# Up-projections of a two-layer decoder trunk: two short matrix products per weight tile or one long one

## The chip, the cores and the metric

The kernel runs on one core of a Trainium2 chip. The metric is the device time of one execution in microseconds, as the median of several. A core has five engines with a queue of instructions each, worked off in order: TensorE (matrix products, and the loading of their stationary operand), VectorE, ScalarE, GpSimd, and SyncE, which here only issues DMAs. Matrix products write to PSUM, which has eight banks of 512 float32 columns on 128 partitions; the other data lie in SBUF.

## The reference

Input is one sequence of 256 tokens with 1024 features, in float32. The trunk is an attention layer, a gated feed-forward layer with a short causal convolution, a second attention layer and a second feed-forward layer, with a final normalisation. The change concerns the feed-forward layers only:

```python
def conv_ffn(h, w_up, conv_w, conv_b, w_down):
    S_ = h.shape[1]
    u = h @ w_up
    up = jnp.pad(u, ((0, 0), (CONV_W - 1, 0), (0, 0)))
    u = conv_b + sum(conv_w[j] * up[:, j:j + S_] for j in range(CONV_W))
    gate, val = jnp.split(u, 2, axis=-1)
    return (jax.nn.silu(gate) * val) @ w_down
...
        x = x + conv_ffn(rmsnorm(x, ffn_norm[l]), w_up[l], conv_w[l], conv_b[l], w_down[l])
```

Here `w_up` is 1024 × 5632 (gate and value, 2816 columns each), `w_down` 2816 × 1024, and the convolution has width 3.

## The kernel before

**Precision.** Each float32 operand of a large product is split into a high part in the matrix unit's rounded float32 format and a low part, the rounded rest. A product is the sum of three: high by high, high by low, low by high. ScalarE makes the high part of a weight (`hi_part`, L177), VectorE the low part by a subtraction (`lo_part`, L185).

**Weights.** They come in 92 units of 128 × 2048 float32, 1 MB each, one DMA per unit from SyncE's queue into one of three buffers (`wr`), from where they are split into one of four pairs of buffers (`wh`, `wl`). `used(i)`, called when the products of unit i are written down, puts the preparation of unit i + 4 on a list: high and low part in two pieces each (four for the first few units of a stage), and after the last low part the DMA for unit i + 3.

**Order.** TensorE's products are written down in the order of the program. Other work is put on a list with due times by `chain(key, (delay, step), ...)`; `tick(ns)` moves a planned clock forward with each product and lets what is due be written down, and `require(key)` writes it down at once where a product needs it. The planned clock is a means to order instructions and nothing that runs on the chip. In the feed-forward layers the framework's scheduler still arranges the instructions of each engine from that order and from their dependences.

**Up-projection.** For each i from 0 to 21 one unit of weights holds, for eight chunks c of 128 input features and two halves j (gate and value), a 128 × 128 block. A step makes 2 × 8 × 3 = 48 products: the weight block is the stationary operand, the input, transposed to features by 256 tokens, the moving one. The result is two halves of 128 × 256, that is one PSUM bank. Steps 0 to 3 (`n_raw`) read the input before it is multiplied by the normalisation's row factors `rb`, and VectorE multiplies their results by `rb` afterwards (`scale`, L714) into an SBUF tile. From step 4 on the input read is the scaled one, `hS`, which `scale_x` makes (L698, L700, L701), and the results are read from PSUM directly. Their banks come from two tags in turn, "u" and "t", of two banks each.

**After the product** (`post`): ScalarE applies the last tap and the bias (`tap2`, L718) into an SBUF tile; VectorE adds the two other taps to it (`taps`, L722 and L724, two of each per step); ScalarE takes the gate's silu (L728), GpSimd multiplies it by the value half (L729), ScalarE and VectorE split the outcome into high and low part (L733, L734). These are the stationary operands of the down-projection, 11 units of weights with products of 512 columns (L588, L589, L593) that accumulate in the four "acc" banks.

The names `turns` and `pairs` are views: a product reads columns t and t + half of its moving operand in turn, and writes them to neighbouring places of PSUM, so that the result lies with the two tokens or features of a pair next to each other as the data are laid out here.

Of the kernel before, what the change touches and what calls it, by code (L numbers as in the profile page):

```python
# [10 lines left out]
AF = mybir.ActivationFunctionType  # L11
ALU = mybir.AluOpType
AX = mybir.AxisListType

P = 128
D = 1024
S = 256
NB = S // P
KC = D // P
# [7 lines left out]
NF = DFF // P  # L27
# [32 lines left out]
def trunk(ctx: ExitStack, tc, x, xw, pos, cpk, fin, sinks, w, out):  # L60
    nc = tc.nc
# [8 lines left out]
    def nm(s):  # L70
        uid[0] += 1
        return f"{s}_{uid[0]}"
# [5 lines left out]
    def spaced(pool, n, dt, tag, name, bufs):  # L78
        return pool.tile([P, n + ROUND], dt, tag=tag, name=name, bufs=bufs)[:, SKIP:SKIP + n]

    def quad(dt=F32R, name="q"):
        return spaced(qd, 4 * S, dt, "q", nm(name), 15).rearrange("p (c t) -> p c t", c=4)

    def mid():
        return wk.tile([P, 512], F32, tag="m2", name=nm("m2"), bufs=6)

    def row3(n=3 * P):
        return wk.tile([P, 3 * P + 8], F32, tag="m3", name=nm("m3"), bufs=8)[:, 4:4 + n]
# [7 lines left out]
    def bank(tag):  # L96
        return ps.tile([P, 512], F32, tag=tag, name=nm(tag), bufs=4 if tag == "acc" else 2)

    def f(ap):
        return ap.bitcast(F32)  # L100
# [7 lines left out]
    def turns(ap):  # L108

        return ap.rearrange("p (a t) -> p t a", a=2)  # L110

    def pairs(ap):
        return ap.rearrange("p (t a) -> p t a", a=2)
# [8 lines left out]
    def run_item(item):  # L122
        put_off.remove(item)
        was, busy[0] = busy[0], True
        item[2]()
        busy[0] = was

    def tick(ns):
        clock[0] += ns
        while put_off and not busy[0]:  # L130
            item = min(put_off, key=lambda t: t[0])
            if item[0] > clock[0]:
                return
            run_item(item)

    def chain(key, *steps, urgent=0):

        def run(k):
            if urgent:
                with tc.high_priority(offset=urgent):  # L140
                    steps[k][1]()
            else:
                steps[k][1]()
            if k + 1 < len(steps):
                put_off.append((clock[0] + steps[k + 1][0], key, lambda: run(k + 1)))
        put_off.append((clock[0] + steps[0][0], key, lambda: run(0)))

    def require(*key):

        while True:  # L150
            mine = [t for t in put_off if t[1] == key]
            if not mine:
                return
            run_item(min(mine, key=lambda t: t[0]))


    wq = {}
# [55 lines left out]
    def used(i):  # L213

        prepare(i + 4)

    def need(i):
        require("w", i)
# [48 lines left out]
    for b in range(NB):  # L267
        t = one.tile([P, NH, HD], F32, name=f"v{b}")
# [12 lines left out]
    def new_hT():  # L281

        return [(quad(), quad()) for _ in range(2)]
# [71 lines left out]
    def hx(hT, c):  # L355
        hi, lo = hT[c // 4]
        return hi[:, c % 4], lo[:, c % 4]
# [306 lines left out]
    def ffn(layer, u_up, u_dn, hT, y, rb, after, tail=None):  # L664
        parts = []

        n_raw = 4
        hS = new_hT()

        def mm(i, up, cs_):  # L670
            need(u_up + i)
            hi, lo = wq[u_up + i]
            for j in range(2):
                o = up[j]
                for c in cs_:
                    if i < n_raw:
                        for b in range(NB):
                            require("x", b, c // 4)
                    else:
                        require("y", c // 2)  # L680
                    s_ = slice((2 * c + j) * P, (2 * c + j + 1) * P)
                    xh, xl = (turns(t) for t in hx(hT if i < n_raw else hS, c))
                    nc.tensor.matmul(pairs(o), hi[:, s_], xh, start=(c == 0), stop=False)  # L683
                    nc.tensor.matmul(pairs(o), hi[:, s_], xl, start=False, stop=False)  # L684
                    nc.tensor.matmul(pairs(o), lo[:, s_], xh, start=False, stop=(c == KC - 1))  # L685
                    tick(3 * 256 / 2.4)

        def scale_x(m):

            c = slice(2 * (m % 2), 2 * (m % 2) + 2)  # L690
            y_, hi, lo = (t[:, c] for t in (y[m // 2], *hS[m // 2]))

            def times():
                for b in range(NB):
                    require("rb", b)
                y4 = y_.rearrange("p c (a t) -> p c a t", a=2)
                r4 = rb.rearrange("p (t a) -> p a t", a=2).unsqueeze(1).to_broadcast([P, 2, 2, P])
                nc.vector.tensor_tensor(out=y4, in0=y4, in1=r4, op=ALU.mult)  # L698

            chain(("y", m), (2000.0 + 1000.0 * m, times), (700.0, lambda: nc.scalar.activation(hi, y_, AF.Copy)),  # L700
                  (600.0, lambda: nc.vector.tensor_tensor(out=lo, in0=y_, in1=f(hi), op=ALU.subtract)))  # L701

        def post(i, up, pq):
            hi, lo = pq[:, 2 * (i % 2)], pq[:, 2 * (i % 2) + 1]
            t = [row3(S) for _ in range(2)]
            gs, h = row3(S), row3(S)
            w0, w1, w2, bb = ([cp[:, CW + (layer * 2 * NF + j * NF + i) * 4 + k:][:, :1] for j in range(2)] for k in range(4))
            us = [mid()[:, :S] for _ in range(2)] if i < n_raw else up

            def scale():  # L710
                for b in range(NB):
                    require("rb", b)
                for j in range(2):
                    nc.vector.tensor_tensor(out=us[j], in0=up[j], in1=rb, op=ALU.mult)  # L714

            def tap2():
                for j in range(2):
                    nc.scalar.activation(t[j], us[j], AF.Identity, scale=w2[j], bias=bb[j])  # L718

            def taps():  # L720
                for j in range(2):
                    nc.vector.scalar_tensor_tensor(out=t[j][:, 1:], in0=us[j][:, :S - 1], scalar=w1[j], in1=t[j][:, 1:],  # L722
                                                   op0=ALU.mult, op1=ALU.add)
                    nc.vector.scalar_tensor_tensor(out=t[j][:, 2:], in0=us[j][:, :S - 2], scalar=w0[j], in1=t[j][:, 2:],  # L724
                                                   op0=ALU.mult, op1=ALU.add)

            def gate():
                nc.scalar.activation(gs, t[0], AF.Silu)  # L728
                nc.gpsimd.tensor_tensor(out=h, in0=gs, in1=t[1], op=ALU.mult)  # L729

            steps = [(200.0, scale), (700.0, tap2)] if i < n_raw else [(200.0, tap2)]
            chain(("p", i), *steps, (400.0, taps), (1600.0, gate),
                  (3400.0, lambda: nc.scalar.activation(hi, h, AF.Copy)),  # L733
                  (450.0, lambda: nc.vector.tensor_tensor(out=lo, in0=h, in1=f(hi), op=ALU.subtract)))  # L734
            parts.append((hi, lo))

        pq = quad()
        ups = [[bank(t)[:, :S] for _ in range(2)] for t in ("u", "acc")]
        for cs_ in (range(4), range(4, KC)):
            for i in range(2):  # L740
                mm(i, ups[i], cs_)
        for i in range(2):
            used(u_up + i)
            post(i, ups[i], pq)
        for m in range(4):
            scale_x(m)
        for i in range(2, NF):
            if i % 2 == 0:
                pq = quad()
            up = bank("acc" if i < 4 else "t" if i % 2 else "u")  # L750
            mm(i, [up[:, :S], up[:, S:]], range(KC))
            used(u_up + i)
            post(i, [up[:, :S], up[:, S:]], pq)

        def wait(i):
            require("p", 2 * i)
            require("p", 2 * i + 1)

        if tail is not None:
            nc.sync.dma_start(fin_t, fin.partition_broadcast(P))  # L760
        dn = Down(u_dn, NF // 2, parts, wait, tail is not None)
        for _ in dn.units(0, NF // 2 - 2):
            pass
        dn.finish(NF // 2 - 2, after, tail)
# [20 lines left out]
    hT = new_hT()  # L785
# [200 lines left out]
    hT = new_hT()  # L986
    y = [quad(F32, "y") for _ in range(2)]
# [13 lines left out]
    def after_f0(b, n):  # L1001
# [3 lines left out]
        raw_feats(b, n, xT_h, ("x", b, n))  # L1005

    ffn(0, U_UP0, U_DN0, hT, y, rb, after_f0)


# [60 lines left out]
    hT = new_hT()  # L1070
    y = [quad(F32, "y") for _ in range(2)]
# [55 lines left out]
    r_t = one.tile([P, 1], F32, name="r_t")  # L1127
    yo = []
    ffn(1, U_UP1, U_DN1, hT, y, rb, after_f1, tail)
    while put_off:  # L1130
        run_item(min(put_off, key=lambda t: t[0]))
# [92 lines left out]
```

## Time and profile before

| | |
|---|---|
| median of 3 runs | 551.83 us (551.73 to 551.88) |
| profiled execution | 551.75 us |
| its span, first to last instruction | 550.0 us |
| mean granted TensorE clock | 0.997 |
| TensorE products busy | 540.9 us, 98% of the span |
| VectorE busy | 423.2 us, 77% |
| ScalarE busy | 371.4 us, 68% |
| GpSimd busy | 117.1 us, 21% |
| DMA | 100.98 MB, 184 GB/s |

A line of the profile names the engine (PE is TensorE's products, PEld its weight loads, DVE VectorE, ACT ScalarE, POOL GpSimd), the program line, the operation and the tiles written and read. Groups give total and mean duration. In a timeline a row begins with start and duration in microseconds, and brackets show how long the engine stood idle before it and what released it. Durations of neighbouring instructions on one engine overlap a little, so the pace of a run of instructions is read from their starts. In the first layer's feed-forward part, products of step 4 begin at about 136.5 us and those of the down-projection at about 233 us; in the second layer these are 389.5 and 486 us.

### The profile page before, as it was taken

To read this page: it belongs to the slowest core of one execution; us is meant where nothing else is said; L and a number is where in the kernel's file an instruction comes from. 1 tells how busy PE (TensorE), PEld (TensorE's weight loads), DVE (VectorE), ACT (ScalarE), POOL (GpSimd) and SP (SyncE) were. 2 spreads that over 40 slices of the span, in tenths; PEclk is the share of its full clock that TensorE was granted. 3 is DMA by queue.
4 is the path that set the end of the run, shared out by engine and by line. 5 is a ranking of instruction groups with operands and counts; after the bars stand their busy time and mean duration, and the time that the engine had idled before them with its cause. 6 is when DMAs were issued, how large, how long until landed. Compare 5 with 4: busy or idle time off the path is not lost.

```text
span 550.0 us, 9980 instructions
## 1 busy us (share of the span) xinstructions
PE 540.9 (98%) x3762; PEld 497.1 (90%) x3762; DVE 423.2 (77%) x901; ACT 371.4 (68%) x732; POOL 117.1 (21%) x156
## 2 busy tenths in 40 slices
PE   9999999999999999999999999999999999999995
PEld 7888888899999999988888887889999999998884
DVE  6799777589798889864468989878888898884414
ACT  6779878579577777754368888677657777764313
POOL 8312001012422333130000121102332332320003
PEclk9999999999999999999999999999999999999998
DMA  8985444432466655566552544242374555666201
GB/s 292 396 285 191 154 153 154 154 130 101 164 229 221 228 197 200 220 230 221 173 217 88 220 153 154 83 148 83 148 265 184 203 200 223 238 240 228 99 0 76
DMA packets 15311, 100.98 MB, mean 184 GB/s; under 512 B 1952, under 2 KB 2080, under 8 KB 3744
## 3 DMA queue, kind: packets, MB, share of 16 engines
q1 hardware_dynamic: 14976, 100.09, 50.2%
q8 instruction: 29, 0.48, 0.3%
q10 hardware_dynamic: 288, 0.26, 0.1%
q14 instruction: 18, 0.15, 0.1%
HBM read 99.30 MB, written 1.05 MB: 182 GB/s over the span
## 4 chain that ended last, share of the span: by engine, by line
PE 87%; DMA 3%; ACT 3%; DVE 3%; issue 1%; POOL 1%; POOLq 0%; DVEq 0%; ACTq 0%
PE acc L588 9%; PE acc L593 9%; PE acc L589 9%; PE u L683 7%; PE u L685 6%; PE u L684 6%; PE t L683 6%; PE t L685 6%; PE t L684 6%; PE acc L366 3%; PE acc L367 3%; PE acc L368 3%; DMA wr<-in_w 3%; DVE wl L185 2%; PE acc L685 2%; PE acc L684 2%
## 5 line engine op out<-in xcount | busy, mean ns | idle before, releaser
L185 DVE TENSOR_TENSOR wl<-wr,wh 128x1024 fp32r<-128x1024 f32 (+1 forms) x190 | 207.2, 1108 | 52.2 <-ACT wh L177 51.7
L177 ACT ACTIVATE wh<-wr 128x1024 fp32r<-128x1024 f32 (+1 forms) x188 | 175.0, 959 | 51.4 <-PE acc L593 43.0
L729 POOL TENSOR_TENSOR m<-m,m 128x256 f32<-128x256 f32 x44 | 71.1, 1617 | 166.7 <-DVE m L724 98.5
L588 PE MATMUL acc<-wh,q 128*128 128x512 f32 x238 | 92.2, 387 | 0.0
L589 PE MATMUL acc<-wl,q 128*128 128x512 f32 x238 | 90.5, 380 | 0.0
L683 PE MATMUL u<-q,wh 128*128 128x256 f32 x320 | 88.3, 277 | 0.0
L684 PE MATMUL u<-q,wh 128*128 128x256 f32 x320 | 88.1, 276 | 0.0
L685 PE MATMUL u<-q,wl 128*128 128x256 f32 x320 | 87.9, 275 | 0.0
L683 PE MATMUL t<-q,wh 128*128 128x256 f32 x288 | 79.2, 275 | 0.0
L684 PE MATMUL t<-q,wh 128*128 128x256 f32 x288 | 79.2, 275 | 0.0
L685 PE MATMUL t<-q,wl 128*128 128x256 f32 x288 | 79.2, 275 | 0.0
L593 PE MATMUL acc<-wh,q 128*128 128x512 f32 x238 | 74.5, 379 | 0.0
L685 PEld LDWEIGHTS u<-q,wl 128*128 128x128 f32 x320 | 61.4, 192 | 0.0
L684 PEld LDWEIGHTS u<-q,wh 128*128 128x128 f32 x320 | 61.4, 192 | 0.0
L683 PEld LDWEIGHTS u<-q,wh 128*128 128x128 f32 x320 | 61.3, 192 | 0.0
L683 PEld LDWEIGHTS t<-q,wh 128*128 128x128 f32 x288 | 55.3, 192 | 0.0
L684 PEld LDWEIGHTS t<-q,wh 128*128 128x128 f32 x288 | 55.3, 192 | 0.0
L685 PEld LDWEIGHTS t<-q,wl 128*128 128x128 f32 x288 | 55.3, 192 | 0.0
L588 PEld LDWEIGHTS acc<-wh,q 128*128 128x128 f32 x238 | 45.0, 189 | 6.7 <-issue 0.9
L593 PEld LDWEIGHTS acc<-wh,q 128*128 128x128 f32 x238 | 45.0, 189 | 6.3
L589 PEld LDWEIGHTS acc<-wl,q 128*128 128x128 f32 x238 | 45.0, 189 | 5.7
L733 ACT ACTIVATE q<-m 128x256 fp32r<-128x256 f32 x44 | 18.1, 415 | 46.6 <-POOL m L729 46.6
(177 smaller groups left out, 1030.1 us busy)
## 6 DMA issues: line engine op xcount, KB each, us to landing
wr<-in_w SPq DMA_DIRECT2D x90, 1024.0 KB, 4.8
first<-in_xw SPq DMA_DIRECT2D x5, 384.0 KB, 5.7
xr<-in_x SPq DMA_DIRECT2D x2, 512.0 KB, 9.7
first<-in_xw SPq DMA_DIRECT2D x1, 768.0 KB, 7.1
fin_t<-in_fin SPq DMA_DIRECT2D x1, 512.0 KB, 5.6
out<-ot SPq DMA_DIRECT2D x1, 512.0 KB, 2.6
first<-in_xw SPq DMA_DIRECT2D x1, 388.0 KB, 3.3
out<-m SPq DMA_DIRECT2D x1, 256.0 KB, 2.0
```

Of the source, the lines that this page charges most:

```text
L177: nc.scalar.activation(wq[i][0][:, c], raws[i][:, c], AF.Copy, **({} if g is None else {"scale": g}))
L185: nc.vector.tensor_tensor(out=wq[i][1][:, c], in0=raws[i][:, c], in1=f(wq[i][0][:, c]), op=ALU.subtract)
L366: nc.tensor.matmul(pairs(o), xh[:, blk(b)], turns(wh), start=(c == 0), stop=False)
L367: nc.tensor.matmul(pairs(o), xh[:, blk(b)], turns(wl), start=False, stop=False)
L588: nc.tensor.matmul(pairs(o), ph[:, blk(b)], turns(hi[:, s_]), start=first, stop=False)
L589: nc.tensor.matmul(pairs(o), ph[:, blk(b)], turns(lo[:, s_]), start=False, stop=False)
L593: nc.tensor.matmul(pairs(o), pl[:, blk(b)], turns(hi[:, s_]), start=False, stop=end)
L683: nc.tensor.matmul(pairs(o), hi[:, s_], xh, start=(c == 0), stop=False)
L684: nc.tensor.matmul(pairs(o), hi[:, s_], xl, start=False, stop=False)
L685: nc.tensor.matmul(pairs(o), lo[:, s_], xh, start=False, stop=(c == KC - 1))
L729: nc.gpsimd.tensor_tensor(out=h, in0=gs, in1=t[1], op=ALU.mult)
L733: (3400.0, lambda: nc.scalar.activation(hi, h, AF.Copy)),
```

## The change

From step 4 on, the moving operand holds the high and the low part of the scaled input side by side: `hS` becomes four tiles of two chunks each, in each chunk 256 high and 256 low columns. For each chunk and half, the high part of the weights meets both in one product of 512 columns, which writes a whole PSUM bank: columns 0 to 255 collect high by high, 256 to 511 high by low. The low part of the weights meets the high input in a product of 256 columns that is added to the first 256. A step has 32 products in place of 48. It takes two banks, one for each half, and the pairs of banks come from "u", "t" and twice from "acc" in turn.

The two halves of a bank have to be summed. ScalarE copies the second 256 columns of both banks to an SBUF tile (`aside`), and VectorE adds the first 256 columns from PSUM to it (`both`). The last tap and the other taps read this tile, where they read PSUM before. Steps 0 to 3 keep their products; the two halves of their scaled result now share one tile of 512 columns, where they had one tile each. The planned clock still moves forward by the same amount for each chunk and half.

```diff
-        hS = new_hT()
+        hS = [quad().rearrange("p c (k t) -> p (c k) t", k=1).rearrange("p (c k) t -> p c k t", k=2) for _ in range(KC // 2)]
+
+        def mm_scaled(i, up):
+            need(u_up + i)
+            hi, lo = wq[u_up + i]
+            for c in range(KC):
+                require("y", c // 2)
+                both = hS[c // 2][:, c % 2]
+                for j in range(2):
+                    s_ = slice((2 * c + j) * P, (2 * c + j + 1) * P)
+
+                    def high():
+                        nc.tensor.matmul(up[j].rearrange("p (k t a) -> p k t a", k=2, a=2), hi[:, s_],
+                                         both.rearrange("p k (a t) -> p k t a", a=2), start=(c == 0), stop=(c == KC - 1))
+
+                    def low():
+                        nc.tensor.matmul(pairs(up[j][:, :S]), lo[:, s_], turns(both[:, 0]), start=False, stop=False)
+
+                    for step in (low, high) if c == KC - 1 else (high, low):
+                        step()
+                    tick(3 * 256 / 2.4)
...
-            y_, hi, lo = (t[:, c] for t in (y[m // 2], *hS[m // 2]))
+            y_, hi, lo = y[m // 2][:, c], hS[m][:, :, 0], hS[m][:, :, 1]
...
-            us = [mid()[:, :S] for _ in range(2)] if i < n_raw else up
+            us = [t[:, j * S:(j + 1) * S] for t in (mid(),) for j in range(2)]
+
+            def aside():
+                for j in range(2):
+                    nc.scalar.activation(us[j], up[j][:, S:], AF.Copy)
+
+            def both():
+                for j in range(2):
+                    nc.vector.tensor_tensor(out=us[j], in0=up[j][:, :S], in1=us[j], op=ALU.add)
...
-            steps = [(200.0, scale), (700.0, tap2)] if i < n_raw else [(200.0, tap2)]
+            steps = [(200.0, scale), (700.0, tap2)] if i < n_raw else [(200.0, aside), (450.0, both), (700.0, tap2)]
...
-            up = bank("acc" if i < 4 else "t" if i % 2 else "u")
-            mm(i, [up[:, :S], up[:, S:]], range(KC))
+            if i < n_raw:
+                up = bank("acc")
+                up = [up[:, :S], up[:, S:]]
+                mm(i, up, range(KC))
+            else:
+                up = [bank(("u", "t", "acc", "acc")[(NF - 1 - i) % 4]) for _ in range(2)]
+                mm_scaled(i, up)
             used(u_up + i)
-            post(i, [up[:, :S], up[:, S:]], pq)
+            post(i, up, pq)
```

More of the change, by code (lines that the diff above doesn't have):

```diff
@@ L675, in mm @@
                 for c in cs_:
[L676 to L680, printed above, removed]
+                    for b in range(NB):
+                        require("x", b, c // 4)
                     s_ = slice((2 * c + j) * P, (2 * c + j + 1) * P)
-                    xh, xl = (turns(t) for t in hx(hT if i < n_raw else hS, c))
+                    xh, xl = (turns(t) for t in hx(hT, c))
                     nc.tensor.matmul(pairs(o), hi[:, s_], xh, start=(c == 0), stop=False)
```

## The prediction

> **What bounds the kernel now.** I read the page first, then the busy time by stage over the two stretches that the change touches (the 18 scaled up-projection steps of each layer), then the timeline of single engines inside them. The rows of stretches give, after the length, the busy time of matrix products, weight loads, VectorE, ScalarE and GpSimd, then TensorE's clock.
>
> ```profile
> PE 540.9 (98%) x3762; PEld 497.1 (90%) x3762; DVE 423.2 (77%) x901; ACT 371.4 (68%) x732; POOL 117.1 (21%) x156
> 136.50:233.00 96.50, 96.50 (x866) 96.50 (x866) 83.56 (x136) 66.39 (x110) 29.45 (x18) 1.00 0.58 208
> 389.50:486.00 96.50, 96.50 (x867) 96.50 (x866) 82.57 (x137) 66.58 (x110) 31.25 (x18) 1.00 0.58 213
> ```
>
> In both stretches TensorE is busy without a gap at full clock and sets the end. VectorE is busy 83.56 of 96.50 us, so it is the next in line. A busy TensorE says little about pace, so the pace comes from starts. First two starts one step apart (48 products of 256 columns), then two starts of down-projection that lie eight weight units, 192 products of 512 columns, apart:
>
> ```profile
> 158.00 0.28 PE L683 MATMUL u<-q,wh 128*128 128x256 f32 x1
> ...
> 163.36 0.28 PE L683 MATMUL t<-q,wh 128*128 128x256 f32 x1
> ...
> 238.22 0.38 PE L588 MATMUL acc<-wh,q 128*128 128x512 f32 x1
> ...
> 279.66 0.38 PE L588 MATMUL acc<-wh,q 128*128 128x512 f32 x1
> ```
>
> A 256-column product costs 5.36 / 48 = 111.7 ns, a 512-column one 41.44 / 192 = 215.8 ns. Two short ones cost 223.4, so one long one in their place is 7.6 ns cheaper. What happens where the two lengths meet shows in two places:
>
> ```profile
> 541.66 0.38 PE L593 MATMUL acc<-wh,q 128*128 128x512 f32 x1
> 541.88 0.27 PE L649 MATMUL u<-wh,q 128*128 128x256 f32 x1
> 541.99 0.28 PE L650 MATMUL u<-wl,q 128*128 128x256 f32 x1
> ...
> 38.00 0.28 PE L459 MATMUL acc<-kd,q 128*128 128x256 f32 x1
> 38.11 0.38 PE L366 MATMUL u<-wh,q 128*128 128x512 f32 x1
> ```
>
> After a long product the next starts 0.22 us later, after a short one 0.11 us later: the length of the earlier product decides, and mixing adds nothing.
>
> **TensorE's term.** Each (chunk, half) of a scaled step had three short products, 335.0 ns. It will have one long and one short, 215.8 + 111.7 = 327.5 ns. That is 7.5 ns, times 16 per step, 18 steps and 2 layers = 576 places: 4.3 us. The columns streamed are the same 768; only a weight load and a product's fixed part go. A step becomes 16 × 327.5 = 5.24 us instead of 5.36. The unknown is the long product's read, which takes the high and the low block of one tile as two runs; all long products of the trace read one block. Bounds: as the down-projection's (215.8), or no cheaper than two short ones (223.4, gain nothing). I take 215.8, since the short products of L649, which read pairs 256 elements apart, keep the same 0.11 us as L683's pairs 128 apart: the read pattern did not matter there.
>
> **What the other engines get.** Each scaled step gains two ScalarE copies out of PSUM and two VectorE additions, and the bias and tap operations read SBUF instead of PSUM. One step of today in VectorE's, ScalarE's and GpSimd's order:
>
> ```profile
> 205.89 0.43 DVE L734 TENSOR_TENSOR q<-m,q 128x256 fp32r<-128x256 f32 x1 [0.68 <-ACT q L733]
> 206.23 0.47 DVE L724 SCALAR_TENSOR_TENSOR m<-t,cp,m 128x254 f32<-128x254 f32 x1
> 206.63 0.47 DVE L722 SCALAR_TENSOR_TENSOR m<-t,cp,m 128x255 f32<-128x255 f32 x1
> 207.02 1.22 DVE L185 TENSOR_TENSOR wl<-wr,wh 128x1024 fp32r<-128x1024 f32 x1
> 208.15 0.47 DVE L724 SCALAR_TENSOR_TENSOR m<-t,cp,m 128x254 f32<-128x254 f32 x1
> 208.54 1.21 DVE L185 TENSOR_TENSOR wl<-wr,wh 128x1024 fp32r<-128x1024 f32 x1
> 209.67 0.48 DVE L722 SCALAR_TENSOR_TENSOR m<-u,cp,m 128x255 f32<-128x255 f32 x1
> 210.83 0.43 DVE L734 TENSOR_TENSOR q<-m,q 128x256 fp32r<-128x256 f32 x1 [0.68 <-ACT q L733]
> ...
> 205.44 0.42 ACT L733 ACTIVATE q<-m 128x256 fp32r<-128x256 f32 x1 [1.29 <-POOL m L729]
> 205.76 1.05 ACT L177 ACTIVATE wh<-wr 128x1024 fp32r<-128x1024 f32 x1
> 206.80 0.42 ACT L728 ACTIVATE m<-m 128x256 f32<-128x256 f32 x1
> 207.13 1.04 ACT L177 ACTIVATE wh<-wr 128x1024 fp32r<-128x1024 f32 x1
> 208.07 1.00 ACT L718 ACTIVATE m<-u,cp 128x256 f32<-128x256 f32 x2
> 210.38 0.42 ACT L733 ACTIVATE q<-m 128x256 fp32r<-128x256 f32 x1 [1.30 <-POOL m L729]
> ...
> 208.79 1.55 POOL L729 TENSOR_TENSOR m<-m,m 128x256 f32<-128x256 f32 x1 [3.39 <-DVE m L724]
> 140.72 0.74 DVE L714 TENSOR_TENSOR m<-acc,rb 128x256 f32<-128x256 f32 x2
> L718 ACT ACTIVATE m<-u,cp x36: 545/552/583, 148.6 to 482.3; 128x256 f32<-128x256 f32 x36
> L718 ACT ACTIVATE m<-m,cp x16: 585/587/597, 123.4 to 397.4; 128x256 f32<-128x256 f32 x16
> ```
>
> VectorE repeats after 210.83 − 205.89 = 4.94 us, with 0.68 us idle: 4.26 us of work. An addition of two 256-column operands, one in PSUM, is L714's case: 0.74 us for two, 0.68 once they overlap their neighbours as the others do. VectorE's work becomes 4.94 us a step, against TensorE's new 5.24: it fits, at 94%. ScalarE works 4.94 − 1.30 = 3.64 us; two copies at L733's pace (205.44 to 205.76, 0.32 each) and 0.04 more for each of the two L718 from SBUF (587 against 552 ns) make 4.36 us. It fits too.
>
> Whether it fits in order is the real question, since each queue is in order and the two wait for each other. The new wait is the addition's on the copies; behind it on VectorE stand the low parts of weights and the taps, and behind those ScalarE's L718 and L728. I follow one step from its first addition. VectorE: additions to 0.68, first L185 to 1.81, tap 2.20, L734 2.54, taps 2.93 and 3.32, second L185 4.45, last tap 4.84. Meanwhile ScalarE runs the two L718 from 0.5, then L733, L177, L728, L177 (0.99 + 0.32 + 1.04 + 0.33 + 0.94), up to 4.1, and the next copies to 4.8: ready when VectorE is. The additions read PSUM and so leave GpSimd's L729 room there. What L729 costs VectorE when they meet:
>
> ```profile
> 228.71 0.74 POOL L729 TENSOR_TENSOR m<-m,m 128x256 f32<-128x256 f32 x1 [3.38 <-DVE m L724]
> 228.86 1.67 DVE L185 TENSOR_TENSOR wl<-wr,wh 128x1024 fp32r<-128x1024 f32 x1 [0.32 <-ACT wh L177]
> ```
>
> GpSimd first: its product takes 0.74 and L185 stretches by 1.67 − 1.21 = 0.46. VectorE first: L729 takes 1.55 (208.79, during L185). In the new order L729 starts 0.64 us after the last tap's start (208.15 to 208.79), ends 0.74 later at 1.38, and the next L185 is due at 0.39 + 0.68 = 1.07: it is held 0.31 us. A step is then 4.94 + 0.31 = 5.25 us on VectorE, just TensorE's 5.24. Bounds: 4.94 if the two never meet; 4.94 + 0.68 + 0.46 = 6.08 if today's idle stays and the full stretch comes on top. I take 5.25, because the additions fall where the idle is now.
>
> **What cushion hides a slower VectorE.** Weights are made four units ahead, k counted from a layer's first up-projection unit:
>
> ```profile
> 144.67 1.22 DVE L185 TENSOR_TENSOR wl<-wr,wh 128x1024 fp32r<-128x1024 f32 x1
> ...
> 147.28 0.28 PE L683 MATMUL u<-q,wh 128*128 128x256 f32 x1
> 148.13 2.35 DVE L185 TENSOR_TENSOR wl<-wr,wh 128x1024 fp32r<-128x1024 f32 x2
> 148.60 0.55 ACT L718 ACTIVATE m<-u,cp 128x256 f32<-128x256 f32 x1
> ...
> 145.90:223.40 77.50, 39.44 (x32) 1.00 0.61 218
> ...
> 222.41 1.07 ACT L177 ACTIVATE wh<-wr 128x1024 fp32r<-128x1024 f32 x1 [0.37 <-PE t L684]
> ```
>
> The last row starts unit 23, when step 19 lets its buffers go. The row above counts 32 low parts before that, two a unit: units 7 to 22. So the L185 at 144.67 finishes unit 6 at 145.89, and TensorE enters step 6 at 147.28: 1.39 us to spare. Unit 7's second low part is the first of the pair at 148.13, done at 149.35, 3.3 us before step 7 at 147.28 + 5.36 = 152.64. Steps 0 to 3 are unchanged, and no addition stands ahead of unit 6, so at the new pace (two steps, 0.24 us) 1.15 us remain. From unit 7 on the cushion is 3.3 us and changes by 5.24 minus VectorE's step. At 5.25 it stays; TensorE never waits. Freed PSUM is no limit: a step now takes two banks, so step i + 4 reuses those of i, 15.7 us after i ends, and the queues run some 7 us behind at worst (step 4 ends at 147.28 − 5.36 = 141.92, its L718 starts at 148.60). Weight DMAs do not change in number:
>
> ```profile
> wr<-in_w SPq DMA_DIRECT2D x90, 1024.0 KB, 4.8
> ```
>
> At 4.8 us to landing with three buffers they keep up with 5.24. The changed bank rotation, the shared tile for both halves and the tile layout cost no instruction.
>
> **Sum.** The profiled execution took 551.75 us for a span of 550.0, close to the median of 551.83. 551.75 − 4.3 = 547.4 us.
>
> **Rivals.**
> *VectorE becomes the bound (other side).* Reading the taps' input from SBUF makes four more VectorE operations a step collide with L729, and today's 0.68 us of waiting for ScalarE stays. For: L729's 1.55 and L185's 1.67, and VectorE's 94%. Against: the walk above. At 5.85 us a step, the middle of 5.62 (idle stays) and 6.08, 15 steps lose 15 × 0.61 − 3.3 = 5.9 us a layer, 11.7 in all: 551.75 − 4.3 + 11.7 = 559 us. It decides from 5.60 us a step on, where 2 × (15 × 0.36 − 3.3) eats the 4.3. The Trainium skill's page "SBUF — State Buffer", section "Who interferes with whom", says that a VectorE instruction with two SBUF inputs contends with a GpSimd instruction that reads SBUF, one with a single SBUF input does not; the two rows agree, and it speaks against moving the taps' input to SBUF.
>
> *The long product is dearer.* Its two-run read brings it to 223.4 ns: no gain, VectorE hidden, 551.8 us. For: no row has such a read. Against: L649.
>
> *The short product gets cheaper.* Its 111.7 is more than half of 215.8. If something it shares with its short neighbours holds it back, and a long neighbour hides that, it can fall to that half, 107.9: a place 323.7, gain 11.3 × 576 = 6.5 us, 545.2 us. Against: the 0.11 us at both junctions. The Trainium skill's page "TensorE: Matmul & The Clock Gate", section "Back-to-back issue gap", gives N/2.4 + 2.5 ns, 109.2 for 256 columns, by which today's place would be 327.6, the new one 325.0, and the gain an estimated 1.5 us (550.3). The row of today says 111.7 and not 109.2, so this gets no chance of its own.
>
> **How the numbers follow.** Kept in full, 547.4 (546.7 to 548.7): 0.49. VectorE partly in the way, 548.7 to 552: 0.14, half of it still faster. VectorE the bound, 552 to 566: 0.22. Dear long product: 0.07. Cheap short product: 0.08. Measurement tells about 0.2%, 1.1 us: faster means under 550.7, slower over 552.9. Faster 0.49 + 0.08 + 0.07 = 0.64; same 0.07 + 0.07 = 0.14; slower 0.22. The range 546.0 to 557.0 leaves out the cheapest corner and the upper half of the VectorE case.
>
> **What would show it.** Right: product starts 0.22 and 0.11 us apart in the new lines, a step 5.24 us, no TensorE idle in up-projection, VectorE near 95% there, low parts still finished over 1 us ahead. Wrong: TensorE idle released by L185 or by an addition, VectorE's step above 5.5 us, L729 or the taps stretched; or long products nearer 0.224 us than 0.216.

## The result, and the profile after

The changed kernel takes 557.23 us, the median of six runs from 555.5 to 560.0, against 551.54 us of the kernel before beside it. The ratio is 1.0112, with an interval of 1.0091 to 1.0134: slower by about 1.1%, where the prediction had 0.8% faster. The profiled execution took 556.2 us for a span of 554.5, 4.5 us more than before. The rows below come from it. One execution in the experiments, the profiled one of the run with the short gate product, had a granted clock of 0.72 and took 733 us; it is left out of the times.

First the page's busy times and its chain that ended last, by engine. The last row is that chain in the kernel before, where products were busy for 540.9 us.

```profile
PE 539.3 (97%) x3186; PEld 479.1 (86%) x3186; DVE 456.2 (82%) x973; ACT 396.3 (71%) x804; POOL 104.6 (19%) x156
...
PE 47%; DVE 28%; ACT 10%; POOL 5%; issue 5%; DMA 3%; SPq 0%; POOLq 0%; DVEq 0%; ACTq 0%
...
PE 87%; DMA 3%; ACT 3%; DVE 3%; issue 1%; POOL 1%; POOLq 0%; DVEq 0%; ACTq 0%
```

There are 576 products fewer, as meant, and TensorE is still busy for 97% of the span. But the chain that ended last runs through TensorE for only 47% of the span now, where it was 87%. VectorE, ScalarE and GpSimd hold 43% of it. TensorE's own rows tell where that bites. These are starts in step 12 of the first layer and of step 13, then the start of each layer's down-projection:

```profile
178.52 0.38 PE L685 MATMUL t<-q,wh 128*128 128x512 f32 x1
178.73 0.27 PE L689 MATMUL t<-q,wl 128*128 128x256 f32 x1
178.84 0.38 PE L685 MATMUL t<-q,wh 128*128 128x512 f32 x1
...
183.76 0.38 PE L685 MATMUL u<-q,wh 128*128 128x512 f32 x1
...
230.92 0.38 PE L588 MATMUL acc<-wh,q 128*128 128x512 f32 x1
...
233.46 0.48 PE L588 MATMUL acc<-wh,q 128*128 128x512 f32 x1 [1.09 <-DVE m L738]
...
235.45 0.48 PE L588 MATMUL acc<-wh,q 128*128 128x512 f32 x1 [1.28 <-DVE m L738]
...
239.00 0.38 PE L588 MATMUL acc<-wh,q 128*128 128x512 f32 x1
...
484.82 0.38 PE L588 MATMUL acc<-wh,q 128*128 128x512 f32 x1
...
488.40 0.48 PE L588 MATMUL acc<-wh,q 128*128 128x512 f32 x1 [2.12 <-DVE m L738]
...
490.39 0.68 PE L588 MATMUL acc<-wh,q 128*128 128x512 f32 x1 [1.29 <-DVE m L738]
490.86 0.63 PE L589 MATMUL acc<-wl,q 128*128 128x512 f32 x1
491.29 0.63 PE L593 MATMUL acc<-wh,q 128*128 128x512 f32 x1
...
495.63 0.38 PE L588 MATMUL acc<-wh,q 128*128 128x512 f32 x1
```

In the up-projection all is as forecast. The long product is followed after 0.21 to 0.22 us, the short one after 0.11, and step 12 takes 183.76 − 178.52 = 5.24 us. From there to the down-projection are nine more steps in 230.92 − 183.76 = 47.16 us, 5.24 each: TensorE never waits in them. Then the first down-projection unit, 24 products of 512 columns and so 5.18 us by the pace of before, takes 239.00 − 230.92 = 8.08 us in the first layer and 495.63 − 484.82 = 10.81 in the second. That is 2.90 and 5.63 us too much, 8.5 together. Against the 4.3 us gained, it leaves the kernel 4.2 us slower, and the span grew by 4.5. The remaining 0.3 us lie elsewhere and were not followed up.

The brackets name what released the waiting products: L738, the new addition. The view of waits says that it was this at all four places:

```profile
PE acc L588 <- DVE m L738: 5.8, 4, 2.1
```

(5.8 us in total, four times, the longest 2.1.) The down-projection needs all four "acc" banks almost at once, and step 19 left its two halves in two of them. Here is VectorE in its steady order, with one row of GpSimd, and the two additions that let the down-projection go on:

```profile
195.46 0.41 DVE L738 TENSOR_TENSOR m<-t,m 128x256 f32<-128x256 f32 x1
195.71 0.73 POOL L759 TENSOR_TENSOR m<-m,m 128x256 f32<-128x256 f32 x1 [4.63 <-ACT m L734]
195.79 1.73 DVE L185 TENSOR_TENSOR wl<-wr,wh 128x1024 fp32r<-128x1024 f32 x1
197.44 0.41 DVE L738 TENSOR_TENSOR m<-t,m 128x256 f32<-128x256 f32 x1
...
199.29 1.21 DVE L185 TENSOR_TENSOR wl<-wr,wh 128x1024 fp32r<-128x1024 f32 x1
...
200.82 0.41 DVE L738 TENSOR_TENSOR m<-u,m 128x256 f32<-128x256 f32 x1
...
233.00 0.41 DVE L738 TENSOR_TENSOR m<-acc,m 128x256 f32<-128x256 f32 x1
...
234.98 0.41 DVE L738 TENSOR_TENSOR m<-acc,m 128x256 f32<-128x256 f32 x1
```

The additions of step 19 end at 233.41 and 235.39, and the two waiting products start 0.05 us later each. Step 19's products had ended at 230.92 − 2 × 5.24 = 220.44, so the addition is 12.56 us behind. Of step 12, whose products end at 183.76, the addition stands at 195.46: 11.70 us behind. VectorE's step is 200.82 − 195.46 = 5.36 us, and so it loses 0.12 a step on TensorE. The larger part of the lag is older:

```profile
147.75 0.75 DVE L738 TENSOR_TENSOR m<-t,m 128x256 f32<-128x256 f32 x2
...
157.06 2.36 DVE L185 TENSOR_TENSOR wl<-wr,wh 128x1024 fp32r<-128x1024 f32 x2
157.34 2.67 POOL L759 TENSOR_TENSOR m<-m,m 128x256 f32<-128x256 f32 x1 [3.88 <-ACT m L758]
160.04 0.42 ACT L763 ACTIVATE q<-m 128x256 fp32r<-128x256 f32 x1 [2.51 <-POOL m L759]
160.76 0.42 DVE L738 TENSOR_TENSOR m<-acc,m 128x256 f32<-128x256 f32 x1 [1.01 <-ACT m L734]
...
179.45 0.42 DVE L738 TENSOR_TENSOR m<-u,m 128x256 f32<-128x256 f32 x1
```

The first row holds step 4's additions, the last row the first addition of step 9. Step 4's products end at 183.76 − 8 × 5.24 = 141.84, step 9's at 168.04: the lag grows from 5.91 to 11.41 us in five steps, 6.34 us of VectorE each. In these steps VectorE isn't full: of the 31.70 us from 147.75 to 179.45 it is busy for 26.89 and waits for the rest. The middle rows show one such loop. GpSimd's gate product starts during two low parts that stand back to back, and takes 2.67 us instead of 0.73. ScalarE's next instruction (L763) waits 2.51 us for it. Behind L763 stands the second copy of the step (L734), and VectorE's addition waits 1.01 us for that.

The busy time by stage shows both phases, and the clock at the two down-projections. Columns are as in the prediction: length, busy time of products, weight loads, VectorE, ScalarE, GpSimd, then the granted clock.

```profile
160.00:185.00 25.00, 25.00 (x155) 22.95 (x154) 20.34 (x36) 17.46 (x33) 4.95 (x5) 1.00 0.47 171
185.00:210.00 25.00, 25.00 (x155) 22.99 (x154) 24.49 (x43) 21.04 (x39) 3.55 (x5) 1.00 0.58 209
210.00:230.90 20.90, 20.90 (x129) 19.25 (x128) 20.90 (x36) 17.61 (x32) 2.92 (x4) 1.00 0.53 189
233.00:237.00 4.00, 2.25 (x9) 1.69 (x10) 4.00 (x9) 3.08 (x7) 0.73 (x1) 1.00 0.77 262
488.00:492.00 4.00, 2.31 (x6) 1.63 (x7) 4.00 (x9) 3.07 (x7) 0.73 (x1) 0.82 0.76 271
492.00:494.40 2.40, 2.40 (x8) 1.87 (x8) 2.40 (x4) 2.11 (x5) 0.73 (x1) 0.59 0.70 230
```

Up to 185 us VectorE is busy 20.34 of 25 us and yet falls behind; from 210 us it is busy without a gap and cannot catch up. In the second layer the two waits cost more than their own length. The clock falls, and products stand 0.43 us apart (490.86 to 491.29) instead of 0.216. The rows give the loss: 0.18 × 4.00 + 0.41 × 2.40 = 1.70 us.

### The profile page after: what moved, and what is told of

Read it like the earlier page. It is cut to its first block, busy times and chain, and to the rows that moved or that the text cites. A ratio compares the mean times of both kernels' runs of the same rounds, so it can differ in the third digit from the quotient of the medians.

```text
span 554.5 us, 8988 instructions
## 1 busy us (share of the span) xinstructions
PE 539.3 (97%) x3186; PEld 479.1 (86%) x3186; DVE 456.2 (82%) x973; ACT 396.3 (71%) x804; POOL 104.6 (19%) x156
## 4 chain that ended last, share of the span: by engine, by line
PE 47%; DVE 28%; ACT 10%; POOL 5%; issue 5%; DMA 3%; SPq 0%; POOLq 0%; DVEq 0%; ACTq 0%
DVE wl L185 11%; PE acc L588 9%; PE acc L593 9%; PE acc L589 9%; DVE m L752 5%; POOL m L759 5%; ACT wh L177 5%; DVE m L754 4%; PE acc L366 3%; DVE m L738 3%; PE acc L367 3%; PE acc L368 3%; DMA wr<-in_w 2%; PE t L538 2%; PE u L515 1%
## 5 line engine op out<-in xcount | busy, mean ns | idle before, releaser
L185 DVE TENSOR_TENSOR wl<-wr,wh 128x1024 fp32r<-128x1024 f32 (+1 forms) x190 | 217.0, 1161 | 35.2 <-ACT wh L177 34.9
L588 PE MATMUL acc<-wh,q 128*128 128x512 f32 x238 | 93.3, 392 | 5.8 <-DVE m L738 5.8
L759 POOL TENSOR_TENSOR m<-m,m 128x256 f32<-128x256 f32 x44 | 54.2, 1233 | 205.6 <-ACT m L734 106.2
L589 PE MATMUL acc<-wl,q 128*128 128x512 f32 x238 | 91.2, 383 | 0.0
L685 PE MATMUL acc<-q,wh 128*128 128x512 f32 x256 | 84.2, 382 | 0.0
L593 PE MATMUL acc<-wh,q 128*128 128x512 f32 x238 | 75.1, 381 | 0.0
L689 PE MATMUL acc<-q,wl 128*128 128x256 f32 x256 | 67.2, 273 | 0.0
L748 ACT ACTIVATE m<-m,cp 128x256 f32<-128x256 f32 x88 | 50.8, 595 | 6.7 <-DVE m L738 5.8
L685 PE MATMUL t<-q,wh 128*128 128x512 f32 x160 | 53.5, 382 | 0.0
L685 PE MATMUL u<-q,wh 128*128 128x512 f32 x160 | 53.5, 382 | 0.0
L685 PEld LDWEIGHTS acc<-q,wh 128*128 128x128 f32 x256 | 47.8, 189 | 5.9
L689 PEld LDWEIGHTS acc<-q,wl 128*128 128x128 f32 x256 | 49.1, 192 | 0.8
L366 PE MATMUL acc<-wh,q 128*128 128x512 f32 x112 | 44.0, 393 | 0.0
L367 PE MATMUL acc<-wl,q 128*128 128x512 f32 x112 | 42.7, 381 | 0.2 <-DVE wl L185 0.2
L368 PE MATMUL acc<-wh,q 128*128 128x512 f32 x112 | 42.6, 380 | 0.0
L689 PE MATMUL u<-q,wl 128*128 128x256 f32 x160 | 42.0, 273 | 0.0
```

The costliest lines, as they stand in the source:

```text
L185: nc.vector.tensor_tensor(out=wq[i][1][:, c], in0=raws[i][:, c], in1=f(wq[i][0][:, c]), op=ALU.subtract)
L366: nc.tensor.matmul(pairs(o), xh[:, blk(b)], turns(wh), start=(c == 0), stop=False)
L367: nc.tensor.matmul(pairs(o), xh[:, blk(b)], turns(wl), start=False, stop=False)
L368: nc.tensor.matmul(pairs(o), xl[:, blk(b)], turns(wh), start=False, stop=(c == KC - 1))
L588: nc.tensor.matmul(pairs(o), ph[:, blk(b)], turns(hi[:, s_]), start=first, stop=False)
L589: nc.tensor.matmul(pairs(o), ph[:, blk(b)], turns(lo[:, s_]), start=False, stop=False)
```

## The experiments

All are edits of the changed kernel but the last. Comparisons are with the kernel before, run beside each.

The traces gave one theory and one rival. Theory: VectorE as a whole is too slow beside GpSimd, and the "acc" banks are only where it shows first. Rival: the down-projection's order of banks alone costs the time.

### Down-projection's first two units by token block

The four products that need step 19's banks come after those that need the others.

```diff
-        for _ in dn.units(0, NF // 2 - 2):
+        for b in range(NB):
+            for i in range(2):
+                for k in range(2):
+                    dn.mm(i, k, b, [(n, slice(0, 512)) for n in range(2)])
+        for i in range(2):
+            used(u_dn + i)
+        for _ in dn.units(2, NF // 2 - 2):
```

> The changed kernel, with the first two weight units of each down-projection worked off by token block: block 0 of both units, then block 1 of both. All products and sums stay. TensorE then wants the two accumulator banks that step 19 used 5.18 us after the down-projection begins instead of 1.30 us after. Theory A (TensorE waits for PSUM banks, and for nothing else): in the first layer the banks are wanted at 230.92 + 5.18 = 236.1 and free at 235.4, in the second at 490.0 and 490.3; the waits of 2.4 and 3.4 us and the clock loss go, about 548 us. Theory B (VectorE has become the bound as a whole, and the bank is only the first thing that comes late): unit 1's low parts, wanted now from 233.5 on, are finished at 235.1 and 238.0, so TensorE waits there instead, and the third unit starts within 0.5 us of the 244.2 us of the changed kernel: 554 to 558 us.

555.07 us, ratio 1.0068 (1.0053 to 1.0083). The waits for additions are gone, and others stand in their place, in the view of waits:

```profile
PE acc L589 <- DVE wl L185: 6.8, 6, 1.4
```

TensorE now waits six times for low parts of weights, which queue on VectorE behind the same work. The third unit begins at 244.68 us, without the edit at 244.18: nothing of the lag is gained. So the bank is only the first thing that comes late. About 2 us are won; the clock did not fall in this kernel's runs (0.996 to 0.998), and the clock loss of the trace above is 1.70 us.

### Where does the cost lie: the old form for the last four steps

Steps 18 to 21 use short products, one bank each from "u" and "t", without copies and additions.

```diff
-            steps = ... [(200.0, aside), (450.0, both), (700.0, tap2)]
+            steps = ... [(200.0, aside), (450.0, both), (700.0, tap2)] if i < N_SHORT else [(200.0, tap2)]
...
+            else:
+                up = bank("t" if i % 2 else "u")
+                up = [up[:, :S], up[:, S:]]
+                mm_short(i, up)
```

> The changed kernel, with steps 18 to 21 of each up-projection as before the change (three short products, one bank of u or t, no copy, no addition). Steps 4 to 17 stay changed. The accumulator banks are last used by step 17, and VectorE has four lighter steps of about 4.3 to 4.9 us in which to catch up before the down-projection. Theory (VectorE's step of 5.36 us against TensorE's 5.24 lets it fall behind to 12.3 us, which the down-projection's start then pays): no TensorE wait at the down-projection, saving of TensorE 14 x 16 x 2 x 7.5 ns = 3.4 us: 548.1 us. Rival (TensorE's loss comes from something else than the last steps, such as order elsewhere in the program): no better than 553 us.

577.09 us, ratio 1.0468 (1.0442 to 1.0494): a miss of both theories, by the design of the edit. Step 18's bank, a "u", had been used by step 17, one step earlier:

```profile
PE t L720 <- DVE m L753: 14.9, 2, 7.7
PE u L720 <- DVE m L753: 7.4, 2, 3.7
```

(L720 is the short product here and L753 the addition. A few products into a "t" bank stand ahead of step 18's "u" in TensorE's order, so the wait is split in two.) In the first layer step 17's last product starts at 210.90 us and the first into the "u" bank at 223.83, 12.9 us later, right after step 17's first addition. A bank that is wanted again one step later pays the whole lag. That confirms the size of the lag, not its cause.

### No copies, no additions

High by high and low by high alone are used; the sum with high by low is left out of the result.

```diff
-            us = [t[:, j * S:(j + 1) * S] for t in (mid(),) for j in range(2)]
+            us = [t[:, j * S:(j + 1) * S] for t in (mid(),) for j in range(2)] if i < n_raw else [u[:, :S] for u in up]
...
-            steps = ... [(200.0, aside), (450.0, both), (700.0, tap2)]
+            steps = ... [(200.0, tap2)]
```

> The changed kernel without the two copies and the two additions per step: the bias and taps read the first half of each bank, so the product of high weights and low input is made and left out of the result. This is TensorE's part of the change alone. Both theories: TensorE's step 5.24 us, VectorE as before at about 4.9 us, no wait at the down-projection: 551.5 - 4.3 = 547.2 us. If it is not below 549 us, the long product or the two banks a step cost something by themselves.

567.35 us, ratio 1.0299 (1.0282 to 1.0316): another miss, and the run that taught most. With less work it is slower. The rows are the busy time of one stage, and GpSimd's gate product with ScalarE's split after it:

```profile
185.00:210.00 25.00, 25.00 (x154) 22.98 (x153) 18.30 (x28) 14.42 (x25) 3.13 (x5) 1.00 0.52 171
...
202.80 0.73 POOL L759 TENSOR_TENSOR m<-m,m 128x256 f32<-128x256 f32 x1 [5.38 <-DVE m L754]
...
203.57 0.42 ACT L763 ACTIVATE q<-m 128x256 fp32r<-128x256 f32 x1 [2.58 <-POOL m L759]
...
208.91 0.74 POOL L759 TENSOR_TENSOR m<-m,m 128x256 f32<-128x256 f32 x1 [5.38 <-DVE m L754]
```

VectorE is busy 18.30 of 25 us, and its step still takes 208.91 − 202.80 = 6.11 us. GpSimd is not held up here (0.73), but the order of the queues makes a loop: last tap, gate product, split, and only then the next step's taps. What an engine can do in a step is set by such a loop as much as by its busy time. The edit changed the scheduler's order, so it does not price the additions.

### The rest of the change without the long products

Two short products into both halves of the bank take the long one's place.

```diff
-                        nc.tensor.matmul(up[j].rearrange("p (k t a) -> p k t a", k=2, a=2), hi[:, s_],
-                                         both.rearrange("p k (a t) -> p k t a", a=2), start=(c == 0), stop=(c == KC - 1))
+                        nc.tensor.matmul(pairs(up[j][:, :S]), hi[:, s_], turns(both[:, 0]), start=(c == 0), stop=False)
+                        nc.tensor.matmul(pairs(up[j][:, S:]), hi[:, s_], turns(both[:, 1]), start=False, stop=(c == KC - 1))
```

> The changed kernel with TensorE's saving taken out: each long product is two short ones into the two halves of the same bank, so a step has 48 products again and takes 5.36 us; copies, additions, banks and VectorE's order stay. This is the other engines' part of the change alone. VectorE's step of 5.36 us now equals TensorE's, so VectorE falls about 11.5 us behind in the first eight steps and no further. Theory (VectorE is the bound): TensorE reaches the down-projection 2.1 us later per layer and finds the work at nearly the same place, so the whole time is near that of the changed kernel, 553 to 556 us, with waits of about 1 us per layer. If the additions cost nothing as long as TensorE is not faster: 551.5 us.

560.46 us, ratio 1.0167 (1.0139 to 1.0195). The direction was right, the size underestimated: 553 to 556 us had been expected, with waits of about 1 us per layer. Waits at the same four places, 3.2 us per layer, stand in it:

```profile
PE acc L588 <- DVE m L738: 6.4, 4, 2.1
```

What the change does to the other engines costs about 9.4 us by itself, and the long products give back some 3 of it in the changed kernel.

### A shorter gate product on GpSimd

GpSimd multiplies 32 of 256 tokens; the rest of the gate product is left out.

```diff
-                nc.gpsimd.tensor_tensor(out=h, in0=gs, in1=t[1], op=ALU.mult)
+                nc.gpsimd.tensor_tensor(out=gs[:, :32], in0=gs[:, :32], in1=t[1][:, :32], op=ALU.mult)
```

> The changed kernel with GpSimd's product of gate and value made for 32 of the 256 tokens, in the place of the gate; the other 224 columns carry the gate alone (that part of the computation is left out). Copies, additions, taps and VectorE's order of instructions in the steady steps stay; the scheduler moves a few in the first ones. Theory (VectorE is late because it and GpSimd share the way to SBUF: GpSimd's 0.73 us hold a low part of weights for 0.52 us in each steady step, and GpSimd's waiting behind low parts makes ScalarE and then VectorE idle in steps 4 to 9): VectorE's step falls from 5.37 to about 4.9 us, the additions' lag at step 18 from 12.4 to under 8 us, no TensorE wait at the down-projection: 547 to 548.5 us. Rival (VectorE and ScalarE are late by their own work and their waits for each other): lag above 10 us, 553 us or more.

547.13 us, ratio 0.992 (0.9903 to 0.9936). VectorE's own work is unchanged, copies and additions are all there, and the whole loss is gone. From its trace only the order of instructions is read. In the steady steps VectorE's queue stands as in the changed kernel: addition, L185, addition, tap, split, two taps, L185, tap. So in these steps it is not another order that brings the gain. VectorE's step and its lag were not measured in this run.

### The gate product on VectorE

Everything is computed; VectorE gets one instruction more a step, GpSimd none.

```diff
-                nc.gpsimd.tensor_tensor(out=h, in0=gs, in1=t[1], op=ALU.mult)
+                nc.vector.tensor_tensor(out=h, in0=gs, in1=t[1], op=ALU.mult)
```

> The changed kernel with the product of gate and value made by VectorE in place of GpSimd. All is computed. VectorE gains one operation of 256 columns a step, 0.34 to 0.39 us, and loses the 0.52 us for which GpSimd holds it, and no chain goes through GpSimd any more. The scheduler's order changes with it. Theory (shared way to SBUF): VectorE's steady step is 4.84 + 0.36 = 5.20 us, just under TensorE's 5.24, and the idle time of steps 4 to 9 goes: about 548 us. Rival (VectorE's work alone is too much): a step of 5.4 us or more and a lag as before, 556 us or more.

547.69 us (547.42 to 547.74), ratio 0.9931 (0.9916 to 0.9945). The busy time of a stage and VectorE's rows one step apart:

```profile
160.00:185.00 25.00, 25.00 (x155) 23.02 (x154) 25.00 (x50) 20.29 (x39) 0.00 (x0) 1.00 0.57 206
...
168.38 0.77 DVE L738 TENSOR_TENSOR m<-t,m 128x256 f32<-128x256 f32 x2
169.04 1.24 DVE L185 TENSOR_TENSOR wl<-wr,wh 128x1024 fp32r<-128x1024 f32 x1
...
172.09 0.44 DVE L759 TENSOR_TENSOR m<-m,m 128x256 f32<-128x256 f32 x1
...
173.56 0.77 DVE L738 TENSOR_TENSOR m<-u,m 128x256 f32<-128x256 f32 x2
```

VectorE now has more to do and never pauses, and its step is 173.56 − 168.38 = 5.18 us: under TensorE's 5.24, so the lag shrinks by 0.06 a step. No L185 is stretched. This version beats both kernels, by 3.7 us the one before and by 9.5 the changed one.

The same with copies and additions placed ahead of other work, so that the two additions stand together in every step. In the first layer of the run above they already did in steps 5 to 16 (the rows marked x2) and stood apart in step 4 and the last five:

```diff
+                with tc.high_priority(offset=40):
                     for j in range(2):
                         nc.scalar.activation(us[j], up[j][:, S:], AF.Copy)
...
+                with tc.high_priority(offset=40):
                     for j in range(2):
                         nc.vector.tensor_tensor(out=us[j], in0=up[j][:, :S], in1=us[j], op=ALU.add)
```

> As the run with the gate's product on VectorE, and the two copies and the two additions of a step are given a higher priority in the scheduler, so that the two additions stand next to each other in VectorE's queue instead of on either side of a low part (2.0 us apart in the changed kernel). Theory: VectorE's work of 5.20 us a step is the same, the second bank of a step comes free 1.6 us earlier: about 547.5 us, no slower than the run without the priority. Rival (the order does not matter as long as VectorE is full): equal to that run.

547.1 us, ratio 0.993 (0.9912 to 0.9948), which can't be told from the run above. Where VectorE keeps up, the order of these few steps made no difference.

### The additions together, the gate product still on GpSimd

The prediction's walk through one step had the two additions next to each other. The last diff on the changed kernel, with GpSimd as it is, makes that part of its order.

> The changed kernel with copies and additions given a higher priority, so that the two additions of a step stand next to each other in VectorE's queue; the gate product stays on GpSimd, everything computed. My prediction's walk had them next to each other and came to 5.25 us a step of VectorE. If the walk was right and only the order that it assumed was not met, VectorE keeps up, no product of the down-projection waits over 0.5 us, and the time is 547 to 549 us. If the walk itself missed the hold of L185 by GpSimd's product, VectorE's step stays at 5.35 us or more, additions end 10 us or more behind the products by step 18, and the time is 554 to 560 us.

581.72 us, ratio 1.0549 (1.0531 to 1.0567): far slower than either side had expected. To have the additions together does not make VectorE keep up. One step of VectorE, ScalarE and GpSimd (lines are two further down than in the changed kernel: L740 is the addition, L761 the gate product, L765 and L766 its split):

```profile
190.63 1.22 DVE L185 TENSOR_TENSOR wl<-wr,wh 128x1024 fp32r<-128x1024 f32 x1
190.96 1.49 POOL L761 TENSOR_TENSOR m<-m,m 128x256 f32<-128x256 f32 x1 [5.02 <-ACT m L760]
192.48 0.42 ACT L765 ACTIVATE q<-m 128x256 fp32r<-128x256 f32 x1 [1.65 <-POOL m L761]
192.93 0.42 DVE L766 TENSOR_TENSOR q<-m,q 128x256 fp32r<-128x256 f32 x1 [1.08 <-ACT q L765]
193.27 0.75 DVE L740 TENSOR_TENSOR m<-acc,m 128x256 f32<-128x256 f32 x2
...
199.77 0.75 DVE L740 TENSOR_TENSOR m<-t,m 128x256 f32<-128x256 f32 x2
```

The step is 199.77 − 193.27 = 6.50 us, though no L185 is stretched. It is the loop of the run without additions again, in full view. The gate product starts 0.33 us into a low part and takes 1.49 instead of 0.73, because VectorE was first. L765 waits for it and L766 for L765. The next additions stand behind L766, and all taps, the silu and the next gate product behind them. In the prediction's walk the split stood behind the additions and the first L185, so this run shares one feature with the walk and is not the walk's own order, which was not run.

### The gate product on VectorE in the kernel before

```diff
-                nc.gpsimd.tensor_tensor(out=h, in0=gs, in1=t[1], op=ALU.mult)
+                nc.vector.tensor_tensor(out=h, in0=gs, in1=t[1], op=ALU.mult)
```

> The kernel before with its gate product (L729) on VectorE instead of GpSimd, everything computed. A control: is the gain of the changed kernel with this move the move's own? Theory (the gain is the long products'): TensorE sets the pace of the kernel before at 5.36 us a step with VectorE at 83.56 of 96.50 us, so the move alone gives nothing: 551.0 to 552.0 us. Rival (the shared way to SBUF costs the kernel before something too, near the down-projections): faster by 1 us or more.

551.62 us, ratio 1.0002 (0.9993 to 1.0012). VectorE takes the extra work within TensorE's 96.50 us, where it was busy 83.56 before:

```profile
136.50:233.00 96.50, 96.50 (x864) 96.47 (x864) 89.73 (x156) 66.72 (x110) 1.12 (x2) 1.00 0.59 208
```

So the move alone gives nothing; the 3.7 us belong to the long products, once nothing takes them back.

## Why the prediction was wrong

**TensorE's term was right.** Step 5.24 us was forecast and 5.24 measured, with 0.22 and 0.11 us at the junctions, and no product in the up-projection waited. With the other engines out of the way the kernel takes 547.1 to 547.7 us; the forecast was 547.4. The rivals of a dearer long and a cheaper short product fall.

**The walk of VectorE's step failed.** It had 4.94 us of work, 0.31 of hold by L729, and "just TensorE's 5.24". Measured in the steady order are 5.36, of which 0.52 are hold: 1.73 against 1.21 for the L185 beside the gate product. The walk's own sum without the hold, 4.84, plus this 0.52 is what the trace has. The hold was sized by the assumption that the additions stand together and give GpSimd room. In the trace they stand 2.0 us apart (195.46 and 197.44), on either side of an L185, and the gate product starts 0.08 us before that L185. Additions together would not have been enough: the run that has them so, with the split ahead of them, takes 6.50 us a step.

**The larger failure is the loop that the walk did not close.** It followed each engine once through a step and asked whether the work fits. It did not follow the gate product back to the next additions. In steps 4 to 9 the step took 6.34 us, above the upper bound of 6.08, with VectorE idle between. Of the 12.56 us of lag at step 19, 5.9 stood at step 4, where the prediction had some 7; 5.5 came up to step 9, and 1.15 in the ten steps after it, at 0.12 each.

**"Freed PSUM is no limit" failed.** The sentence compared step i + 4 with step i, 15.7 us apart, and that pair did hold: at 12.6 us of lag no up-projection product waited. It left out the consumer after the last step. The down-projection takes all four "acc" banks in its first unit, and step 19's additions were 12.56 us late where the prediction had some 7 us "at worst".

**The cushion of weights was misread, on the safe side.** It was counted to the start of a step, but a unit's second piece is needed only half a step, 2.6 us, later: step 19's low parts end 1.4 us after its first product, and nothing waits for them. With VectorE this slow the low parts would have been the next to come late, as the run by token block shows.

**The rival had the right engine and the wrong place.** VectorE did become the bound, the gate product (L729, now L759) has a part in it, and the rival's 559 us is near the 557.2. But it let low parts stall the up-projection from 5.60 us a step on; what happened is a lag that grows unseen for 18 steps and is paid at the next stage. That its price fell out similar is chance: the real one is 8.5 us in the first units of two down-projections, 1.70 of it clock. Its chance of 0.22 was too low: VectorE at 94% with two-way waits among three queues deserved more, and the range's upper end of 557.0 cut it in half.

Nor did the collisions come where the rival had them, with the four tap operations a step that now read SBUF. These keep their length, here for one line (L754 has 479 ns); today's rows in the prediction have 0.47 us:

```profile
L752 DVE SCALAR_TENSOR_TENSOR m<-m,cp,m 128x255 f32<-128x255 f32 x88 | 41.1, 474 | 4.8 <-ACT m L748 4.7
```

The rule quoted beside the rival fits the instruction that is held. The Trainium skill's page "SBUF — State Buffer", section "Who interferes with whom", says that a VectorE instruction with two SBUF inputs contends with a GpSimd instruction that reads SBUF. The trace agrees: L185 takes 1.73 for 1.21, and the gate product up to 2.67 for 0.73. But L185 had two SBUF inputs before the change as well (1.67 in the prediction's rows), and then it was mostly GpSimd that was held, with 29.45 us for 18 gate products in the prediction's first stretch. The change altered who starts first, and left VectorE less time to spare. With the gate product on VectorE no L185 takes longer than 1.35 us.

**What stays open.** The runs with a short gate product and with one on VectorE take away the hold of 0.52 us and the loop through GpSimd together. How much of the 12.6 us of lag each would make alone was not separated; the run without copies and additions shows that a loop through GpSimd, with neither L185 nor the gate product stretched, suffices to make a kernel slower, if in another order of instructions.

## What to carry to other kernels

When work goes to an engine at 80 to 90% busy, do not stop at its sum of durations: close the loop of waits from one step to the next through every in-order queue, and take that as the step. A follower that is slower than the leader by 0.1 us a step costs nothing until something wants its buffers, so look at the first consumer after the stage, not only at the buffers inside it. And a helper engine that shares a resource with the bound may be worth emptying: 0.33 us more of work on VectorE was cheaper than 0.73 us of help from GpSimd.

## What the runs showed of the hardware

The clock fell after one pair of waits and not after another. At the first layer's down-projection TensorE waited 1.09 and 1.28 us and kept its clock (1.00). At the second it waited 2.12 and 1.29 us, and then the clock fell, for a loss of 1.70 us; in shorter stretches the trace has it at 0.50 from 490.60 to 493.80. At half clock a loss of 1.70 us takes 3.4 us. The Trainium skill's page "TensorE: Matmul & The Clock Gate", section "What's actually happening", has a free-running window of 3413 ns and half the clock after an idle one. The length agrees with the trace. "Idle" does not: the longest wait is 2.12 us, so any stretch of 3.4 us before the fall had products in it. How many are enough to keep the clock is not shown.

The times of the changed kernel go with its mean clock, 555.5 to 556.2 us at 0.994 or 0.995 and 558.3 to 560.0 us at 0.987 to 0.989, which would fit more of such falls in the longer ones; no trace shows them.

GpSimd's product takes 0.73 us when it starts before a two-input VectorE instruction, 1.49 when it starts during one, and 2.67 during two back to back, which suggests that it was not let in between them.
